# Modulation and head folds of an encoder layer issued at other places: second modulation in the Fourier stage, one side step per place

## The chip, the core and the metric

The kernel runs on one core of one Trainium2 chip. The metric is the device time of one execution in microseconds. The five engines each run their own list of instructions in order: TensorE (PE, with its weight loads as PEld), VectorE (DVE), ScalarE (ACT), GpSimd (POOL) and SyncE (SP), which issues most of the DMA transfers. All products are 32-bit; most are computed as three TensorE products of high and low parts (a value is split in two by a ScalarE copy and a VectorE subtraction).

## The reference

Two sequences of 1024 rows and 1024 columns go through one encoder layer each, with the same weights and a conditioning vector of their own:

```
mod = silu(c) @ w_ada + b_ada            # six vectors: shift, scale, gate, twice
h   = rmsnorm(x, g_mix) * (1 + sc1) + sh1
z   = h @ w_in                           # 256 q, 128 kv, 64 k_pe, 512 Fourier columns
y_mla  = attention of 4 heads from the normed q and kv latents (w_uq, w_ukv, rotary k)
y_four = real part of a 2-D DFT over sequence and 64 channels of each of 8 groups, times w_four
x   = x + ga1 * (concat(y_mla, y_four) @ w_out)
h2  = rmsnorm(x, g_ffn) * (1 + sc2) + sh2
x   = x + ga2 * ((silu(h2 @ w_gate) * (h2 @ w_up)) @ w_down)
y   = rmsnorm(x, g_final)
```

What the change touches is `mod` (an 1024 x 6144 product with two rows of c), and the weights that are prepared on the chip: `w_out` times the value part of `w_ukv` for each head, and the table of the channel DFT times the Fourier columns of `w_in`.

## The kernel before

**Prologue (0 to about 57 us).** Folded weights are made: `fold_q` (L219) for the scores, `fold_out` (L232) for the output (per head two 128 x 512 products, scaled by VectorE, stored by GpSimd's DMA queue to `wo_d`), `fold_pe` (L243). Between them run the first modulation's eight chunks: `mod_load` (L174) loads 128 rows of `w_ada` (1 MB), `mod_mm` (L182) multiplies them with silu(c), kept in `scT`, as four 32-column products. `mod_vecs` (L194) turns the summed rows into column vectors `s1`, `sh1`. The two loads of `w_out` rows for `fold_out` (L465, L470) lie between the chunk loads; the second goes to the tile `hl1`, which later takes half of `wz`.

**Stage 1 (to about 286 us).** It runs over eight pairs of row tiles (two sequences, four pairs each). `norm` (L348) loads and scales the rows (four x buffers, so two pairs), `flip` (L363) transposes them and applies shift and scale, `zproj` (L395) projects to the latents, `latents` (L425) transposes and stores them, `evenodd` (L381) and `fourier_in` (L438) make the Fourier columns with the channel table `wcs`, which `prep_wcs` (L330) makes in eight blocks of 128 rows. In `pair` (L515) the flips of the next pair are interleaved. Table blocks 0 to 3 are made ahead of the first `zproj`, blocks 4 to 7 and `norm(1)` behind it (L500 to L506).

At three places of each pair the generator `extras` (L262) is advanced; a step ends at each `yield`. It loads and multiplies the eight chunks of the gates (`cols1`), computes `small_weights`, multiplies `w_out`'s Fourier rows with the small weights and the gates into `wm_d` and `wn_d` (ten products, one step each), and at last the eight chunks of the second modulation (`cols2`), closed by `mod_vecs` for `s2`, `sh2`. Pair 0 advances it once, pairs 1 to 6 two steps at each place. Chunks pass through two 1 MB tiles (`wada`, L172).

**Fourier stage (to about 380 us).** `dft` (L619) multiplies with cosine and sine tables, `prep_wm` (L653) loads and splits `wm_d`, `fourier_out` (L689) makes the output rows in four steps per sequence and stores them to `fo_d`; then `stage3_loads` (L578) prepares the attention, which uses `wo_d` (L921) and, at its end, `s2` and `sh2` (L789). The feed-forward part begins near 890 us.

The order of the instructions on each engine is not that of the source: the tile layer places them by its own estimate of when operands and buffers are ready, and adds the waits. PSUM has eight banks of 128 x 512, shared by all products of a stage.

Of the kernel before, what the change touches and what calls it, by code (L numbers as in the profile page):

```python
# [12 lines left out]
F32 = mybir.dt.float32  # L13
# [37 lines left out]
def hybrid_encoder_kernel(ctx: ExitStack, tc: tile.TileContext, a: dict):  # L51
# [53 lines left out]
    ga_d = dram.tile([P, 512], F32, name="ga_d")  # L105
    wq_d = dram.tile([P, 2, 768], F32, name="wq_d")
# [20 lines left out]
    def rows(j, u):  # L127
        return slice(512 * u + P * j, 512 * u + P * j + P)

# [6 lines left out]
    with ExitStack() as st:  # L136
# [30 lines left out]
        nc.scalar.activation(scT[:, :, 0:2], cT, AF.Silu)  # L167

# [25 lines left out]
        def mod_vecs(mr, bcol, gi, sv, shv):  # L194
            pt = bank().rearrange("p (a b) -> p a b", a=4)
            for c in range(4):
                nc.tensor.transpose(pt[:, c, :], mr[:, c * P : (c + 1) * P], ident)
            for s in range(2):
                for j in range(2):
                    nc.vector.tensor_tensor(  # L200
                        out=shv[s][:, 4 * j : 4 * j + 4], in0=pt[:, :, 32 * j + s],
                        in1=bT[:, bcol + 4 * j : bcol + 4 * j + 4], op=ALU.add)
                    nc.vector.tensor_tensor(
                        out=sv[s][:, 4 * j : 4 * j + 4], in0=pt[:, :, 64 + 32 * j + s],
                        in1=bT[:, bcol + 8 + 4 * j : bcol + 12 + 4 * j], op=ALU.add)
                nc.vector.tensor_scalar(out=sv[s], in0=sv[s], scalar1=1.0, scalar2=None, op0=ALU.add)
                nc.vector.tensor_tensor(out=sv[s], in0=sv[s], in1=gT[:, gi, :], op=ALU.mult)

# [23 lines left out]
        def fold_out(i, wo2, wuvT, gq):  # L232
            for b in range(2):
                h = 2 * i + b
                for g in range(2):
                    gs = slice(512 * g, 512 * g + 512)
                    ps = bank()
                    nc.tensor.matmul(ps, wuvT[:, h, :], wo2[:, b, gs], start=True, stop=True)
                    so = stile("so")
                    nc.vector.tensor_scalar(out=so, in0=ps, scalar1=gq[:, 2:3], scalar2=None, op0=ALU.mult)  # L240
                    nc.gpsimd.dma_start(wo_d[:, h, gs], so)
# [20 lines left out]
        def extras():  # L262


            cols1, cols2 = [(2 * D, D), (5 * D, D)], [(3 * D, 2048)]
            wt = mod_load(0, cols1, wada_tile())
            yield
            wo4 = []
            for c in range(NC):
                nxt = mod_load(c + 1, cols1, wada_tile()) if c + 1 < NC else None  # L270
                mod_mm(1, c, wt)
                if c + 1 == NC:
                    wo4.append(wo_load(2, wada_tile()))
                    bga = stile("bga")
                    nc.sync.dma_start(bga, a["bga"])
                wt = nxt
                yield
# [4 lines left out]
            wo4.append(wo_load(3, wada_tile()))  # L282
            wo4 = [t.rearrange("p a b -> p (a b)").rearrange("p (a b) -> p a b", a=2) for t in wo4]
            yield
            for g in range(2):
# [5 lines left out]
                for p in range(5):  # L291
# [171 lines left out]
        wuvT = w.tile([P, HEADS, KVL], F32, tag="ll", name="wuvT", bufs=2)  # L463
        nc.sync.dma_start(wuvT, a["wuvT"])
        wo2 = wo_load(0, wide("hf", (P, 2, D)))  # L465
        mod_mm(0, 0, wt[0])
# [3 lines left out]
        wo2 = wo_load(1, wide("hl1", (P, 2, D)))  # L470
        wpe = w.tile([P, 2, HEADS * ROPE], F32, tag="lh", name="wpe", bufs=2)
        nc.sync.dma_start(wpe, a["wpe"])
# [3 lines left out]
        fold_out(1, wo2, wuvT, gq)  # L476
        fold_pe(wpe, gq)
# [5 lines left out]
        nc.sync.dma_start(bT, a["bT"])  # L483
        nc.sync.dma_start(gT, a["gT"])
# [25 lines left out]
        def extra(k, n):  # L510
            if k <= 6:
                for _ in range(n):
                    next(more, None)

        def pair(k):  # L515
# [11 lines left out]
            extra(k, 2 if k else 0)  # L527
            fourier_in(k, 0)
            latents(k, 1)
            extra(k, 2 if k else 1)  # L530
# [872 lines left out]
```

## Time and profile before

| | |
|---|---|
| median of 3 runs | 2242.17 us (2239.56 to 3430.17) |
| profiled execution | 2243.11 us |
| its span | 2241.3 us |
| TensorE busy | 93% |
| VectorE, ScalarE, GpSimd busy | 63%, 41%, 36% |
| mean granted TensorE clock | 0.967 |
| DMA, mean over the span | 165 GB/s |

The profile is of one execution. A busy share is an average over stages with different limits, so the lines shown below are cut by stretches of time. A line of a group of instructions gives the kernel line, engine, operation, tiles and shape, count, then the busy time in us, the mean of one in ns, and the idle time of the engine before them with what ended it. A line of the timeline gives start, duration, engine, line, operation and tiles, with the idle time before it in brackets. A line of the chain that ended last gives start, duration and what was waited for. The table of stretches gives, for each, its length, their sum, the busy time of each engine with its number of instructions, the granted TensorE clock, the DMA engines' busy share and GB/s. f32 matrix products of two passes are counted as two records.

### The profile page before, as it was taken

Reading aid. Unit: us, or ns where it says so; the run is one execution under the profiler, and the core shown is the slowest. Engines: PE = TensorE matmul, PEld = TensorE weight load, DVE = VectorE, ACT = ScalarE, POOL = GpSimd, SP = SyncE. Lnnn points to the kernel's source line nnn. Section 1 sums busy time; section 2 is a strip of 40 time slices with the busy share of each in tenths; the row PEclk is TensorE's granted clock in tenths of the full one; section 3 lists DMA queues with packets and bytes.
Section 4 is the critical chain, followed back from the end, with each engine's and each line's share of the span. In section 5 each row is a group of like instructions: output and inputs, shape, how many; then the busy total and the mean of one; then the engine's idle time right before and its main releaser. Section 6 shows DMA issues by size and latency. Waiting matters only on the chain.

```text
span 2241.3 us, 28903 instructions
## 1 busy us (share of the span) xinstructions
PE 2084.9 (93%) x10096; PEld 1692.1 (75%) x10096; DVE 1400.8 (63%) x2086; ACT 907.8 (41%) x1774; POOL 814.8 (36%) x1005
## 2 busy tenths in 40 slices
PE   5888999899999895999999999997999999999994
PEld 2666767788888784788888888885778888888883
DVE  3545565766676663776776767667566666655575
ACT  1644542555564455333332336443332332334442
POOL 1433400111223202777877730114555454410124
PEclk7999999999999997999999999999999999999997
DMA  9477546333344237454555468764333232245654
GB/s 377 162 227 222 178 154 225 91 86 86 98 133 139 97 132 228 157 176 164 194 173 184 175 201 295 230 213 159 113 118 118 94 118 94 96 154 197 222 196 141
DMA packets 183362, 370.80 MB, mean 165 GB/s; under 512 B 18928, under 2 KB 60400, under 8 KB 180144
## 3 DMA queue, kind: packets, MB, share of 16 engines
q1 hardware_dynamic: 167712, 314.68, 42.1%
q0 software_dynamic: 15504, 54.28, 7.5%
q8 instruction: 79, 1.29, 0.2%
q14 instruction: 67, 0.55, 0.1%
HBM read 257.02 MB, written 111.87 MB: 165 GB/s over the span
## 4 chain that ended last, share of the span: by engine, by line
PE 77%; DMA 7%; DVE 5%; POOL 4%; ACT 3%; issue 2%; SPq 0%; DVEq 0%; POOLq 0%; ACTq 0%
PE bank L71 21%; PE bank L73 20%; PE bank L72 20%; PE gb L71 2%; PE gb L72 2%; PE gb L73 2%; PE ppt L881 2%; DMA wada<-in_w_ada_dram 2%; PE ps_s L858 1%; PE bank L186 1%; PE ps_s L859 1%; PE ps_s L860 1%; PE ps_s L856 1%; PE ps_s L857 1%; DMA hc_d<-hcb 1%
## 5 line engine op out<-in xcount | busy, mean ns | idle before, releaser
L71 PE MATMUL bank<-H,wh 128*128 128x512 f32 x1232 | 494.3, 401 | 13.8 <-DVE val L125 6.0
L73 PE MATMUL bank<-H,wl 128*128 128x512 f32 x1232 | 487.7, 396 | 0.5 <-DVE wl L61 0.5
L72 PE MATMUL bank<-H,wh 128*128 128x512 f32 x1232 | 485.0, 394 | 0.0
L125 DVE TENSOR_TENSOR val<-bank,val 128x512 f32<-128x512 f32 x260 | 177.1, 689 | 212.0 <-PE bank L73 210.8
L61 DVE TENSOR_TENSOR wl<-draw,wh 128x512 fp32r<-128x512 f32 x308 | 213.5, 731 | 127.8 <-ACT wh L60 127.5
L71 PEld LDWEIGHTS bank<-H,wh 128*128 128x128 f32 x1232 | 232.7, 189 | 70.6 <-DVE val L125 7.3
L73 PEld LDWEIGHTS bank<-H,wl 128*128 128x128 f32 x1232 | 232.3, 189 | 61.4 <-DVE wl L61 1.2
L72 PEld LDWEIGHTS bank<-H,wh 128*128 128x128 f32 x1232 | 232.8, 189 | 55.2
L60 ACT CAST wh<-draw 128x512 fp32r<-128x512 f32 x308 | 179.3, 619 | 216.4 <-PE bank L72 173.1
L125 POOL TENSOR_TENSOR val<-val 128x512 f32<-128x512 f32 x58 | 79.9, 1383 | 507.0 <-DVE val L1227 251.3
L60 ACT CAST wh<-val 128x512 fp32r<-128x512 f32 x176 | 109.0, 622 | 361.3 <-PE bank L72 330.5
L72 PE MATMUL bank<-wl,wh 128*128 128x512 f32 x616 | 242.6, 394 | 8.9 <-DVE wl L61 8.8
L61 DVE TENSOR_TENSOR wl<-val,wh 128x512 fp32r<-128x512 f32 x176 | 193.9, 1104 | 88.0 <-ACT wh L60 87.2
L71 PE MATMUL bank<-wh 128*128 128x512 f32 x616 | 241.8, 393 | 4.5 <-ACT wh L60 4.5
L73 PE MATMUL bank<-wh,wl 128*128 128x512 f32 x616 | 241.4, 392 | 0.0
L60 ACT CAST wh<-rgu 128x512 fp32r<-128x512 f32 x132 | 81.8, 621 | 204.8 <-PE bank L72 202.0
L122 POOL TENSOR_TENSOR val<-rgu 128x512 f32<-128x512 f32 x88 | 121.2, 1379 | 98.7 <-DMA rgu<-in_wgu_dram 86.3
L72 PEld LDWEIGHTS bank<-wl,wh 128*128 128x128 f32 x616 | 116.7, 189 | 36.7 <-DVE wl L61 12.4
L71 PEld LDWEIGHTS bank<-wh 128*128 128x128 f32 x616 | 116.7, 190 | 29.6 <-ACT wh L60 5.4
L122 POOL TENSOR_TENSOR val<-rgu,val 128x512 f32<-128x512 f32 x88 | 132.4, 1505 | 7.5 <-DVE wl L61 0.7
L73 PEld LDWEIGHTS bank<-wh,wl 128*128 128x128 f32 x616 | 116.8, 190 | 24.3
L122 POOL TENSOR_TENSOR val<-val 128x512 f32<-128x512 f32 x89 | 119.6, 1360 | 1.3
(274 smaller groups left out, 3973.6 us busy)
## 6 DMA issues: line engine op xcount, KB each, us to landing
rgu<-in_wgu_dram SPq DMA_DIRECT2D x88, 512.0 KB, 4.6
draw<-s_d SPq DMA_DIRECT2D x154, 256.0 KB, 4.0
s_d<-val POOLq DMA_DIRECT2D x88, 256.0 KB, 3.7
draw<-t_d SPq DMA_DIRECT2D x88, 256.0 KB, 4.3
s_d<-val SPq DMA_DIRECT2D x66, 256.0 KB, 3.1
draw<-in_w_down_dram SPq DMA_DIRECT2D x66, 256.0 KB, 4.5
wada<-in_w_ada_dram SPq DMA_DIRECT2D x13, 1024.0 KB, 7.4
xt<-in_x_dram SPq DMA_DIRECT2D x16, 512.0 KB, 8.4
```

The lines of the kernel that those rows point to most:

```text
L60: here["a"] = nc.scalar.copy(hi, src).ins
L61: here["v"] = nc.vector.tensor_tensor(out=lo, in0=src, in1=rd(hi), op=ALU.subtract).ins
L71: nc.tensor.matmul(out, lh, rh, start=first, stop=False, skip_group_check=cont)
L72: nc.tensor.matmul(out, lh, rl, start=False, stop=False, skip_group_check=cont)
L73: nc.tensor.matmul(out, ll, rh, start=False, stop=last, skip_group_check=cont)
L122: eng.tensor_tensor(out=out, in0=x, in1=y, op=ALU.subtract)
L125: eng.tensor_tensor(out=out, in0=x, in1=y, op=ALU.add)
L186: nc.tensor.matmul(mods[key][32 * j : 32 * j + 32, :], scT[:, c, :], wt[:, j, :], start=(c == 0), stop=(c == NC - 1))
L856: nc.tensor.matmul(o, qa[0][:, us], lat[0][:, 0, gs], start=True, stop=False)
L857: nc.tensor.matmul(o, qa[0][:, us], lat[1][:, 0, gs], start=False, stop=False)
L858: nc.tensor.matmul(o, qa[1][:, us], lat[0][:, 0, gs], start=False, stop=False)
L881: nc.tensor.transpose(pt[:, c, :], p[:, (4 * g + c) * P : (4 * g + c + 1) * P], ident)
```

## The change

The second modulation leaves `extras`. Its eight chunks are loaded and multiplied in the Fourier stage, two after each of the first sequence's four `fourier_out` steps, through four tiles of its own; `scT` is stored to DRAM in the prologue and loaded again there, as are the two small tables `bT`, `gT`. `mod_vecs` becomes a function of both stages and runs after the second `dft`.

`fold_out` now takes one head. Heads 0 and 1 are folded in the prologue, as one load; heads 2 and 3 become the first steps of `extras`, in pair 0, with `wuvT` kept in another tile, and their stores go over SyncE's queue. `extras` is advanced by one step at each of the three places of every pair; two of the `wm` products make one step. All eight table blocks and `norm(1)` stand ahead of the first `zproj`, `wz_split(4)` behind the first flips, `fold_pe` and the loads of `wpe`, `bT`, `gT` earlier.

```diff
+        nc.gpsimd.dma_start(sc_d, scT)
...
-        def fold_out(i, wo2, wuvT, gq):
-            for b in range(2):
-                h = 2 * i + b
-                for g in range(2):
...
-                    nc.gpsimd.dma_start(wo_d[:, h, gs], so)
+        def fold_out(h, wo2, wuvT, gq):
+            for g in range(2):
...
+                (nc.gpsimd if h < 2 else nc.sync).dma_start(wo_d[:, h, gs], so)
...
         def extras():
-            cols1, cols2 = [(2 * D, D), (5 * D, D)], [(3 * D, 2048)]
+            cols1 = [(2 * D, D), (5 * D, D)]
+            wo2 = wo_load(1, wada_tile().rearrange("p a b -> p (a b)").rearrange("p (a b) -> p a b", a=2))
+            yield
+            fold_out(2, wo2, wuvT, gq)
             wt = mod_load(0, cols1, wada_tile())
+            yield
+            fold_out(3, wo2, wuvT, gq)
             yield
...
-                    yield
-            wt = mod_load(0, cols2, wada_tile())
-            yield
-            for c in range(NC):
-                nxt = mod_load(c + 1, cols2, wada_tile()) if c + 1 < NC else None
-                mod_mm(2, c, wt)
-                wt = nxt
-                yield
-            mr = mod_row(2)
-            yield
-            mod_vecs(mr, 24, 1, s2, sh2)
+                    if p % 2 == 1:
+                        yield
             yield
...
-        wuvT = w.tile([P, HEADS, KVL], F32, tag="ll", name="wuvT", bufs=2)
+        wuvT = w.tile([P, HEADS, KVL], F32, tag="gah1", name="wuvT")
...
         fold_out(0, wo2, wuvT, gq)
-        wo2 = wo_load(1, wide("hl1", (P, 2, D)))
...
+        fold_out(1, wo2, wuvT, gq)
+        fold_pe(wpe, gq)
...
-        wz_split(4, wz1)
-        mod_vecs(mod_row(0), 0, 0, s1, sh1)
+        mod_vecs(mod_row(0), bank, bT, gT, 0, 0, s1, sh1)
...
+        for g in range(4):
+            flip(0, g)
+        wz_split(4, wz1)
+        norm(1)
         nc.sync.dma_start(ropec, a["ropec"])
         nc.sync.dma_start(ropes, a["ropes"])
-        for g in range(4):
-            flip(0, g)
-        for i in range(4):
-            prep_wcs(i, wf[0])
+        for i in range(8):
+            prep_wcs(i, wf[i // 4])
         zproj(0, 0)
         evenodd(0)
-        for i in range(4, 8):
-            prep_wcs(i, wf[1])
-        norm(1)
...
-            extra(k, 2 if k else 0)
+            next(more, None)
...
         zsplit(1)
+        scT = wa.tile([P, NC, 32], F32, name="scT2")
+        nc.sync.dma_start(scT, sc_d)
+        bT = wa.tile([P, 48], F32, name="bT2")
+        nc.sync.dma_start(bT, a["bT"])
+        gT = wa.tile([P, 2, NC], F32, name="gT2")
+        nc.sync.dma_start(gT, a["gT"])
+        chunks = {}
+
+        def mod2(c):
+            if c + 3 < NC and c >= 0:
+                mod2_load(c + 3)
+            if c >= 0:
+                if c == 0:
+                    chunks["ps"] = bank2()
+                wt = chunks.pop(c)
+                for j in range(4):
+                    nc.tensor.matmul(chunks["ps"][32 * j : 32 * j + 32, :], scT[:, c, :], wt[:, j, :],
+                                     start=(c == 0), stop=(c == NC - 1))
+
+        def mod2_load(c):
+            chunks[c] = wa.tile([P, 4, 512], F32, tag="wada2", name="wada2", bufs=4)
+            nc.sync.dma_start(chunks[c], a["w_ada"][c * P : (c + 1) * P, 3 * D : 3 * D + 2048].rearrange("p (j n) -> p j n", n=512))
+
+        for c in range(3):
+            mod2_load(c)
         for s in range(2):
             for j in (1, 2, 3, 0):
                 fourier_out(s, abn, j)
                 if j == 1:
                     dc_prep(s, abn)
+                if s == 0:
+                    n = (1, 2, 3, 0).index(j)
+                    mod2(2 * n)
+                    mod2(2 * n + 1)
             if s == 0:
+                mr = wa.tile([P, 512], F32, name="modrow2")
+                nc.vector.tensor_copy(mr, chunks.pop("ps"))
                 abn = dft(1)
                 prep_wm(1)
+                mod_vecs(mr, bank2, bT, gT, 24, 1, s2, sh2)
                 early.close()
```

More of the change, by code (lines that the diff above doesn't have):

```diff
@@ L128, in rows, with mod_vecs @@
         return slice(512 * u + P * j, 512 * u + P * j + P)
+    def mod_vecs(mr, bank, bT, gT, bcol, gi, sv, shv):
+        pt = bank().rearrange("p (a b) -> p a b", a=4)
+        for c in range(4):
+            nc.tensor.transpose(pt[:, c, :], mr[:, c * P : (c + 1) * P], ident)
+        for s in range(2):
+            for j in range(2):
+                nc.vector.tensor_tensor(
+                    out=shv[s][:, 4 * j : 4 * j + 4], in0=pt[:, :, 32 * j + s],
+                    in1=bT[:, bcol + 4 * j : bcol + 4 * j + 4], op=ALU.add)
+                nc.vector.tensor_tensor(
+                    out=sv[s][:, 4 * j : 4 * j + 4], in0=pt[:, :, 64 + 32 * j + s],
+                    in1=bT[:, bcol + 8 + 4 * j : bcol + 12 + 4 * j], op=ALU.add)
+            nc.vector.tensor_scalar(out=sv[s], in0=sv[s], scalar1=1.0, scalar2=None, op0=ALU.add)
+            nc.vector.tensor_tensor(out=sv[s], in0=sv[s], in1=gT[:, gi, :], op=ALU.mult)
     zpool = ExitStack()
@@ L192, in mod_row @@
             return mr
[L194 to L207, printed above, removed]
         def fold_loads():
@@ L526, in pair @@
                 flip(k + 1, 3)
-            extra(k, 2 if k else 0)
+            next(more, None)
             fourier_in(k, 0)
             latents(k, 1)
-            extra(k, 2 if k else 1)
+            next(more, None)
             fourier_in(k, 1)
```

37 lines of the change are left out of this document (16 added, 21 removed).

## The prediction

> **What bounds the kernel now.** I read the page first, then busy time by stage, then TensorE's idle times, then the chain that ended last and the SyncE queue around them.
>
> ```profile
> span 2241.3 us, 28903 instructions
> PE 2084.9 (93%) x10096; PEld 1692.1 (75%) x10096; DVE 1400.8 (63%) x2086; ACT 907.8 (41%) x1774; POOL 814.8 (36%) x1005
> PE   5888999899999895999999999997999999999994
> ```
>
> TensorE is busy for 93% of the span, so a change that leaves its work alone can win only idle time and slow-clock time. The edit lies in the first eight slices (stage 1 up to about 286 us, the Fourier stage up to 380 us). Per stage:
>
> ```profile
> core 0: us, PE busy (x) PEld busy (x) DVE busy (x) ACT busy (x) POOL busy (x), PEclk, DMA share, GB/s
> 12.00:49.00 37.00, 21.70 (x81) 5.41 (x81) 10.99 (x16) 4.08 (x6) 6.83 (x15) 0.75 1.02 418
> 286.00:302.00 16.00, 14.49 (x96) 12.56 (x95) 14.64 (x32) 11.95 (x29) 0.00 (x0) 1.00 0.54 170
> 302.00:337.00 35.00, 34.64 (x146) 22.77 (x146) 23.86 (x49) 11.12 (x21) 0.00 (x0) 1.00 0.35 129
> ```
>
> To 49 us the DMA engines are saturated (share 1.02, 418 GB/s). After that TensorE is the bound, except in a few holes; the Fourier stage (302 to 337) has 0.4 us of idle TensorE and free DMA (129 GB/s). The holes, in brackets the idle time and what ended it:
>
> ```profile
> 75.77 0.66 PE L374 MATMUL bank<-ident,xt 128*128 128x128 f32 x2 [9.67 <-DVE wcs_l L343]
> 158.83 0.69 PE L374 MATMUL bank<-ident,xt 128*128 128x128 f32 x2 [6.92 <-DVE xt L360]
> 207.49 1.26 PE L186 MATMUL bank<-wada,scT 128*32 128x512 f32 x8 [4.31 <-DMA wada<-in_w_ada_dram]
> 213.80 1.06 PE L186 MATMUL bank<-wada,scT 128*32 128x512 f32 x8 [1.54 <-DMA wada<-in_w_ada_dram]
> 251.07 0.63 PE L197 MATMUL bank<-ident,modrow 128*128 128x128 f32 x4 [1.15 <-DVE modrow L191]
> 276.11 0.74 PE L431 MATMUL bank<-ident,lat 128*128 128x128 f32 x4 [1.94 <-DVE lat L416]
> 407.00 0.80 PE L856 MATMUL ps_s<-lat,qa 128*128 128x512 f32 x1 [5.53 <-ACT qa L60]
> ```
>
> Three of them leave TensorE slow behind them, by the granted clock (the last but two number):
>
> ```profile
> 77.00:78.60 1.60, 1.60 (x9) 1.55 (x8) 0.86 (x7) 1.11 (x3) 0.00 (x0) 0.53 0.05 14
> 160.00:164.50 4.50, 4.50 (x13) 2.71 (x12) 1.69 (x6) 2.60 (x6) 1.33 (x6) 0.57 0.60 160
> 406.00:413.00 7.00, 5.42 (x18) 4.44 (x19) 6.23 (x15) 3.56 (x9) 0.73 (x1) 0.51 0.21 61
> ```
>
> **The change part by part.** The sum is made against the profiled execution: 2243.11 us, a span of 2241.3 and 1.8 around it; the median shown, 2242.17, is 0.9 lower.
>
> *Prologue and pair 0.* The last modulation chunk of the prologue is awaited, and the first head folds run under it:
>
> ```profile
> 25.71 20.41 DMA wada<-in_w_ada_dram
> wo_d<-so POOLq DMA_DIRECT2D x8, 256.0 KB, 7.4
> L238 PE MATMUL bank<-wide,wuvT 128*128 128x512 f32 x16 | 9.3, 733 | 1.0 <-DMA wide<-in_w_out_dram 1.0
> L377 ACT ACTIVATE hf<-bank,sh,s 128x256 f32<-128x256 f32 x8 | 4.3, 575 | 9.7 <-PE bank L374 9.7
> L60 ACT CAST hh<-hf 128x512 fp32r<-128x512 f32 x4 | 2.6, 639 | 0.0
> L60 ACT CAST wz_h<-wide 128x896 fp32r<-128x896 f32 x2 | 1.8, 932 | 0.0
> L337 ACT CAST wcs_h<-bank 128x256 fp32r<-128x256 f32 x16 | 5.2, 403 | 0.1
> L342 ACT CAST wcs_h<-bank 128x24 fp32r<-128x24 f32 x8 | 1.4, 189 | 1.1 <-DVE wcs_l L338 1.0
> 71.47 1.09 ACT L356 ACTIVATE junk<-xt 128x1024 bf16<-128x1024 f32 x1
> 164.30 0.20 PE bank L72
> 83.01 0.44 PE bank L431 x4
> 83.44 0.87 PE bank L374 x8
> 84.07 0.37 PE L71 MATMUL bank<-wcs_h,eoh 128*128 128x280 f32 x1
> ```
>
> Taken out of the saturated stretch: one of two loads of w_out (2 x 1024 floats on 128 partitions, 1.05 MB) and four of eight 0.26 MB stores, 2.1 MB at 418 GB/s, 5.0 us, less 0.3 for the new store of scT (0.13 MB): 4.7. If the stores only overlapped the end, 2.5. I take 4, so ScalarE's first hf starts about 4 earlier, near 47.
>
> The 9.67 us hole is an order: the second square of norm(1) starts at 71.47 behind kv, which waits for GpSimd's reciprocal root; xt is scaled after it and flip(1) waits. In the changed program both squares stand ahead of kv and in the middle of the table's copies, and all eight table blocks precede the first projection. What is late next is the projection itself, which needs a PSUM bank that table block 0 releases. From 47: eight hf of 0.575, four hh of 0.64 and a wz copy of 0.93 (8.1), six table copies of 0.40 (2.4), two squares (2.1), two small copies (0.4), by the groups of ScalarE from 49 to 77 us in the fence: 60.0. Then 24 projection matmuls every 0.2 us (4.9), half a flip (0.9), the second projection (4.9), a latent flip and the other half (1.3), the first moved head fold (a quarter of 9.3, 2.3): fourier_in starts at 74.3 against 84.07, and the second fold takes another 2.3 right behind. Gain 7.5. The copy of kv and GpSimd's root still precede hf of pair 1, but that pair is due only after fourier_in. I take 7. Bounds: a loss of 2.1 (4.6 of folds exposed, only 2.5 won) and a gain of 11 (folds at full clock, hole fully closed).
>
> *One step per place, pairs 1 to 6.* Each place had two chunk steps, now one, so a chunk load has about twice the time. The SyncE queue is in order:
>
> ```profile
> 144.41 0.32 SPq L281 DMA_DIRECT2D ga_d<-modrow  x1
> 146.79 0.62 SPq L354 DMA_DIRECT2D xt<-in_x_dram  x1
> 148.43 6.13 DMA xt<-in_x_dram
> 206.47 7.29 DMA wada<-in_w_ada_dram
> DMA to landing us min/median/max: 3.8/5.3/12.8
> ```
>
> The xt of the fifth pair is issued at 146.79, behind ga_d and four latent stores, and flip waits 6.92 us for it. In the changed program that load stands ahead of the third pair's first ckv store, and ga_d a pair further back. So the 6.92 goes, and with it the slow clock: 1.2 us from 158.83 to 160 at half (0.6) and 4.5 at 0.57 (1.9): 9.4 in all. I take 9; bounds 0 (the load ends up late again) and 9.4. Each remaining chunk load is issued one to two places ahead of its use; landing takes 3.8 us at least, 5.3 in the median, 12.8 at most, and a place about 9 (some 20 of them from the fourier_in at 84 to the hole at 276), so I price these loads at 0, and at 4 if the longest meets a single place.
>
> The TensorE page of the Trainium skill ("TensorE: Matmul & The Clock Gate", Part 1) says that after an idle window of about 3.4 us the array runs at half rate until one busy window has passed. The 0.57 row agrees. Its reverse speaks against this change: by that page a newly opened hole would be charged about 1.7 us on top, as an estimate (half of 3.4).
>
> *Second modulation moved to the Fourier stage.* Stage 1 loses 32 matmul pairs and their waits:
>
> ```profile
> L186 PE MATMUL bank<-wada,scT 128*32 128x512 f32 x64 | 8.5, 615 | 5.9 <-DMA wada<-in_w_ada_dram 5.8
> ACT wm L60 <- DMA wraw<-wm_d: 1.6, 1, 1.6
> ```
>
> The 8.5 us of matmuls and 0.6 of transposes go from a TensorE-bound stretch into another: 0. The waits 4.31, 1.54 and 1.15 go: 7.0. The 1.94 in the last pair stays. In the new place 8.4 MB enter a stretch (286 to 337) that moves about 7.2 MB: 15.6 MB in 51 us is 306 GB/s, under 418. Tight is the start: four chunks (4.2 MB) beside the 2.7 MB of 286 to 302 need 431 GB/s, and chunk 0 stands on the SyncE queue ahead of the second four wm loads, for which ScalarE already waits 1.6 us; 1.05 MB at 418 is 2.5 us. TensorE enters fourier_out at 302 just behind wm. Chunks 4 to 7 are issued when the chunk four earlier is used and needed two fourier_out groups (some 14 us) later, more than 12.8. The three small loads (scT, bT, gT) wait there too; SyncE holds fo stores behind a chunk's wait only for the few matmuls before it. Twelve small VectorE instructions and one copy (about 2 us) fit in 11 idle us of 35. I charge 2; bounds 0 and 8 (wm 2.5 and its shadow, two chunk waits).
>
> "DMA: Bandwidth & Descriptors" of the Trainium skill ("Where 436 GB/s comes from") gives about 358 GB/s as what memory grants one core. The 418 row goes past it with one core alone, so the measurement decides; by 358 the first 16 us would need 19.3 and the sum would be some 3 us higher.
>
> *Attention start.* Nothing is edited there, but the order changes. Now SyncE issues two 1 MB latents ahead of the third wo_d load, and ScalarE's wv copy waits for it in front of the exponentials:
>
> ```profile
> 396.06 6.96 DMA wvr<-wo_d
> ```
>
> In the changed program the third load stands between the two latents and ScalarE meets it later. The hole of 5.53 and the clock behind it (5.42 busy at 0.51: 2.7) are 8.2. I take 4; bounds 0 and 8. The feed-forward order is the same on every engine: 0.
>
> Sum: -7 -9 -7 +2 -4 = -25. Span 2216, time 2218 against the profiled run, 2217 against the median: 1.1% faster, inside the 2% (45 us) that a measurement of this kernel can about tell from no change.
>
> **The rivals.**
> *The holes close only in part.* TensorE's order is denser and ScalarE, VectorE and GpSimd's root become what it waits for; pair 0 and the attention start give nothing and the Fourier stage costs 3. For it: the ScalarE chain I worked out for pair 0 has no slack before 60. Against: VectorE is busy 31.5 of 68 us from 77 to 145, as the row of that stretch shows:
>
> ```profile
> 77.00:145.00 68.00, 67.78 (x410) 51.05 (x409) 31.53 (x75) 36.90 (x90) 28.31 (x62) 0.99 0.59 192
> ```
>
> Time: -9 -7 +3 = -13, 2229.
> *All holes close*: -11 -9.4 -7 -8 = -35, 2207.
> *Slower: the Fourier stage waits for chunks.* Chunks 4 to 7 are issued only once a chunk is used, in the same queue as fo stores and wm loads. If landing took the longest seen, 12.8, plus the 5 us that 2 MB ahead cost at 418 GB/s, each would come 4 after the 14 us between issue and use; with 2 of slow clock behind each, four of them cost 24, and the wm loads 8: 32 against 27 won elsewhere, +5, 2247. It decides from a landing of about 17 us per chunk on. Against: the DMA share of 0.35 there.
> *The change doesn't do what it says*: the xt load or a wada load is held up behind another store, and the hole reappears in another pair: -25+16 = -9, 2233.
>
> **How the numbers follow.** Forecast 2217: 0.55. Partly closed, 2229: 0.22. All closed, 2207: 0.12. Fourier stage waits, 2247: 0.06. Hole moves, 2233: 0.05. The forecast's own spread is about 2211 to 2224. The range 2204 to 2234 takes in all but the slow rival and tails on both sides, some 0.15. Faster by over 2% means under 2197, beyond every hole of the sum: 0.04; slower by over 2% (2287) needs 70 us of new waits: 0.03; within: 0.93.
>
> **What would show it.** Right: no idle of several us before the flips of pairs 1 and 4; no TensorE wait for wada after pair 3; fourier_in of pair 0 starting near 74; stage 1 ending near 254 (the 9.1 us of moved TensorE work left it too) and the Fourier stage 9 to 11 us longer. Wrong: rows of TensorE waiting for wada in the Fourier stage, or for wm behind wraw above 3 us; a hole over 6 us in pair 0; the 5.53 us hole of the attention start unchanged.

## The result and the profile after

The changed kernel takes 2210.91 us (median of 4 runs, 2209.74 to 2212.84); the kernel before, run beside it, 2242.17 us (median of 3 runs, 2239.56 to 2243.57; a fourth run of 3430.17 us was slow and is left out, so the upper end that the table of before gives is not of these three). The ratio is 0.9863 with a 95% interval of 0.9844 to 0.9883: 1.4% faster, which is inside the 2%. The forecast was 2217 us, the range 2204 to 2234. In the profiled executions the span fell by 31.0 us where the sum had 25.

The head of the page of the changed kernel:

```profile
span 2210.3 us, 28901 instructions
PE 2076.3 (94%) x10096; PEld 1688.5 (76%) x10096; DVE 1403.0 (63%) x2086; ACT 908.9 (41%) x1774; POOL 819.9 (37%) x1002
```

TensorE has the same number of instructions and 8.6 us less busy time: part of the gain is not idle time at all. To see where it lies, the next two fences mark the same five places in both kernels' timelines of TensorE (start, duration, what it is): the first projection of pair 1, the first matmul of the Fourier stage, of the attention and of the output projection, and the last flip of h ahead of the feed-forward. Before:

```profile
93.63 0.36 PE L71 MATMUL bank<-wz_h,hh 128*128 128x448 f32 x1
...
285.68 0.39 PE L71 MATMUL bank<-tb,zh 128*128 128x258 f32 x1 [1.02 <-ACT zh L60]
...
380.62 0.39 PE L71 MATMUL gb<-wq_h,ql 128*128 128x256 f32 x1 [0.88 <-DVE ed L125]
...
455.46 0.47 PE L71 MATMUL gb<-wv,o 128*128 128x512 f32 x1
...
889.97 1.94 PE L786 MATMUL pht<-ident,xn 128*128 128x128 f32 x8 [7.64 <-DVE xn L776]
```

After, with the waits of TensorE that are left up to the attention (in brackets the idle time and what ended it):

```profile
56.41 0.61 PE L71 MATMUL bank<-wz_h,hh 128*128 128x448 f32 x1 [2.21 <-DVE wcs_l L339]
72.71 0.40 PE L71 MATMUL bank<-wcs_h,eoh 128*128 128x280 f32 x1 [0.84 <-ACT hf L373]
79.11 0.63 PE L427 MATMUL bank<-ident,lat 128*128 128x128 f32 x4 [3.05 <-DVE lat L412]
88.86 0.36 PE L71 MATMUL bank<-wz_h,hh 128*128 128x448 f32 x1
...
238.07 0.63 PE L427 MATMUL bank<-ident,lat 128*128 128x128 f32 x4 [1.44 <-DVE lat L412]
246.49 0.39 PE L71 MATMUL bank<-tb,zh 128*128 128x258 f32 x1 [1.02 <-ACT zh L60]
...
350.15 0.58 PE L71 MATMUL gb<-wq_h,ql 128*128 128x256 f32 x1 [1.60 <-DVE ed L126]
364.54 1.94 PE L901 MATMUL ppt<-ident,p 128*128 128x128 f32 x8 [2.75 <-DVE p L890]
378.87 0.79 PE L876 MATMUL ps_s<-lat,qa 128*128 128x512 f32 x1 [4.24 <-ACT qa L60]
...
426.62 0.47 PE L71 MATMUL gb<-wv,o 128*128 128x512 f32 x1
...
862.76 1.94 PE L806 MATMUL pht<-ident,xn 128*128 128x128 f32 x8 [5.84 <-DVE xn L796]
```

From one mark to the next, in us, beside what the sum had for that stretch:

| stretch | before | after | difference | forecast |
|---|---|---|---|---|
| start to pair 1 (prologue, pair 0) | 93.63 | 88.86 | -4.8 | -7 |
| pair 1 to the Fourier stage | 192.05 | 157.63 | -34.4 | -25.1 (-9, -7, -9.1 moved) |
| Fourier stage | 94.94 | 103.66 | +8.7 | +11.1 (9.1 moved, +2) |
| attention, to the first output projection | 74.84 | 76.47 | +1.6 | -4 |
| to the last flip of h | 434.51 | 436.14 | +1.6 | 0 |
| feed-forward | 1351.3 | 1347.5 | -3.8 | 0 |
| span | 2241.3 | 2210.3 | -31.0 | -25 |

So the total was near, but made of errors that cancel in part: stage 1 won 9 us more than forecast, the prologue 2 less, and the attention start did not win the 4 that were expected.

Each column is one execution, and unchanged code does not always take the same time. By the runs below that leave a stretch as it was, the first row is 87.4 to 90.1 us with the changed code and 93.6 to 95.1 with that of before, and the fourth 74.7 to 76.5 and 74.5 to 75.7. So the 1.6 us that the attention start seems to lose are not shown to be a loss, and differences of 1 to 2 us in the first row mean little.

The same stretches by windows (span of the window, then busy time of TensorE, its weight loads, VectorE, ScalarE, GpSimd, then clock, DMA share, GB/s), before:

```profile
93.63:285.68 192.05, 174.91 (x1015) 135.18 (x1013) 95.06 (x202) 88.92 (x222) 77.17 (x173) 0.96 0.65 206
285.68:380.62 94.94, 92.19 (x432) 65.14 (x433) 65.21 (x132) 34.87 (x75) 0.00 (x0) 1.00 0.50 176
```

and after:

```profile
88.86:246.49 157.63, 154.79 (x946) 128.47 (x944) 93.61 (x189) 88.52 (x222) 77.83 (x168) 1.00 0.67 199
246.49:350.15 103.66, 100.54 (x501) 67.00 (x501) 66.84 (x145) 35.45 (x75) 0.00 (x0) 1.00 0.69 244
```

From pair 1 on stage 1 now keeps TensorE busy for 154.79 of 157.63 us at full clock. The Fourier stage has 3.1 us of idle TensorE against 2.8 before: the eight chunk loads cost it nothing that can be seen. But TensorE's busy time in stage 1 fell by 20.1 us, and what moved is only 8.3: 0.6 of transposes and the chunks' matmuls, 7.7 by their own window after:

```profile
246.49:350.15 103.66, 7.70 (x64) 1.67 (x64) 1.00 0.69 244
```

### The profile page after: what moved, and what is told of

Same layout as the page of the kernel before. It is cut to its first block, busy times and chain, and to the rows that moved or that the text cites. A ratio compares the mean times of both kernels' runs of the same rounds, so it can differ in the third digit from the quotient of the medians.

```text
span 2210.3 us, 28901 instructions
## 1 busy us (share of the span) xinstructions
PE 2076.3 (94%) x10096; PEld 1688.5 (76%) x10096; DVE 1403.0 (63%) x2086; ACT 908.9 (41%) x1774; POOL 819.9 (37%) x1002
## 4 chain that ended last, share of the span: by engine, by line
PE 78%; DMA 6%; POOL 4%; DVE 4%; ACT 4%; issue 3%; SPq 0%; DVEq 0%; POOLq 0%; ACTq 0%
PE bank L71 21%; PE bank L73 21%; PE bank L72 20%; PE gb L71 2%; PE gb L72 2%; PE gb L73 2%; PE ppt L901 2%; DMA wada<-in_w_ada_dram 1%; DMA x<-in_x_dram 1%; PE ps_s L878 1%; PE ps_s L879 1%; PE ps_s L880 1%; PE ps_s L876 1%; DMA hc_d<-hcb 1%; PE ps_s L877 1%
## 5 line engine op out<-in xcount | busy, mean ns | idle before, releaser
L126 POOL TENSOR_TENSOR val<-val 128x512 f32<-128x512 f32 x58 | 81.3, 1409 | 498.8 <-DVE val L1247 329.9
L61 DVE TENSOR_TENSOR wl<-rgu,wh 128x512 fp32r<-128x512 f32 x132 | 116.4, 882 | 8.0 <-ACT wh L60 7.9
```

What stands on the lines that cost most here:

```text
L61: here["v"] = nc.vector.tensor_tensor(out=lo, in0=src, in1=rd(hi), op=ALU.subtract).ins
L126: eng.tensor_tensor(out=out, in0=x, in1=y, op=ALU.add)
```

## The experiments

**Where did 12 us of busy time go?** Slow clock is one answer (0.96 before, 1.00 after). Another stands in TensorE's timeline of the first pairs, which the prediction did not read. One such row of before and the window of the eight chunks of the gate columns (their instructions alone: span, TensorE, weight loads, clock, DMA):

```profile
121.03 1.05 PE L186 MATMUL bank<-wada,scT 128*32 128x512 f32 x4
99.00:134.00 35.00, 13.36 (x64) 2.02 (x64) 1.00 0.74 244
```

A chunk's four matmuls (x8) write 32 rows each and run side by side, 1.06 us for all. In before a chunk came by two loads, and with two steps per place the order of the program issues most chunks as two halves with other work between. Each half (x4) takes 1.05 us too. Run *b_onedma* loads each chunk by one DMA, so the four matmuls stay together:

```
         def mod_load(c, cols, wt):
+            if len(cols) == 2:
+                nc.sync.dma_start(
+                    wt.rearrange("p (k j) n -> p k j n", k=2),
+                    a["w_ada"][c * P : (c + 1) * P, :].rearrange("p (k t j n) -> p k t j n", k=2, t=3, j=2)[:, :, 2])
+                return wt
```

> The kernel before, with each chunk of the first pair's later modulation (gate and feed-forward gate columns) loaded by one DMA instead of two, so that its four matmuls stay together; nothing else is changed. Theory (split chunks): before executes these 8 chunks in 13 bursts, and a burst of half a chunk takes 1.05 us like a whole one (1.06), so 5 bursts or about 5 us go: 2238 us (2236 to 2239), and the bursts of half a chunk between 107 and 133 us are gone from TensorE's rows. Rival (the 6 us that the change won beyond the forecast came from the prologue and pair 0, and split chunks cost nothing because the two halves of the array are filled otherwise): within 1 us of before, 2242.

Measured: 2236.95 us, ratio to before 0.9987 (0.9978 to 0.9997), 2.9 us faster. The chunks' window and the wait that follows later:

```profile
93.00:134.00 41.00, 8.32 (x64) 1.36 (x64) 1.00 0.72 234
...
206.19 1.93 PE L191 MATMUL bank<-wada,scT 128*32 128x512 f32 x8 [7.83 <-DMA wada<-in_w_ada_dram]
```

The same 64 instructions take 8.32 us instead of 13.36: 5.0 us, as the theory said. Of this 3.5 came back some 70 us later: the wait for the second modulation's first chunk grew from 4.31 to 7.83 us. On the other side the second chunk is not awaited any more (1.54 us in before) and no slow clock follows the last latents (1.00 from 272 to 276), so that the Fourier stage starts 4.7 us earlier. The changed kernel issues all chunks whole (8.5 us for 64) and has no such wait left to grow. It still loads each of them by two DMAs; which part of the change keeps them together was not tried by itself. The Trainium skill, "TensorEngine Tiling (Array Packing)", Key Properties, says that tiles of the array can load and multiply in parallel; the trace agrees for the four that stand together (1.06 us), and shows that here two alone took as long (1.05 us).

**Is the fifth pair's hole SyncE's order?** Run *b_xt_early* is the kernel before with the loads of x split from `norm` and, for pairs 3 to 7, issued at the start of `pair(k)`:

```
         def pair(k):
+            if 0 < k < nk - 2:
+                norm_load(k + 2)
             if k > 0:
                 zproj(k, 0)
```

> The kernel before, with the loads of x for pairs 3 to 7 issued at the start of the pair that is two ahead of them instead of at its end; nothing else is changed. Theory (SyncE's order): the 6.92 us wait of the fifth pair's flip for xt goes and the slow clock behind it (2.5 us): 9.4 us faster, 2233 us (2232 to 2235). Rival (the transfers only trade places, and what stood ahead, the ga_d store and the w_out load, becomes late instead): a wait of several us shows elsewhere before 215 us, 2239 to 2243.

Measured: 2236.72 us, 0.9979 (0.9970 to 0.9988), 4.7 us faster. The flip does not wait any more, but the chunk does:

```profile
152.72 1.29 PE L383 MATMUL bank<-ident,xt 128*128 128x128 f32 x8
...
204.77 1.93 PE L186 MATMUL bank<-wada,scT 128*32 128x512 f32 x8 [9.97 <-DMA wada<-in_w_ada_dram]
```

The cause of the hole is confirmed; but the wait for the chunk grew by 5.7 us, and the Fourier stage starts only 5.1 us earlier. That suggested a floor: a chunk that lands at 205 to 207 us however early TensorE is. Run *b_onedma_xt* has both edits and tests it.

> The kernel before with both edits that were tried alone: one DMA per chunk of the first pair's later modulation, and the loads of x issued a pair earlier. Theory (a floor: the first chunk of the second modulation is issued on SyncE's queue behind the wm_d stores, at 199 to 203 us, and lands at 205 to 207 however early TensorE comes): the wait for it grows to 11 to 14 us, stage 1 ends no more than 6 us earlier than before, 2234 to 2237. Rival (the gains add: 3.8 and 4.4 us at the end of stage 1 in the single runs, 8 or more together): the wait stays under 9 us and the time is 2229 to 2232.

Measured: 2231.12 us, 0.9948 (0.9933 to 0.9963), 11.7 us faster; the Fourier stage starts at 274.97, 10.7 earlier than before (4.7 and 5.1 in the single runs).

```profile
198.88 1.94 PE L191 MATMUL bank<-wada,scT 128*32 128x512 f32 x8 [9.02 <-DMA wada<-in_w_ada_dram]
```

The floor falls: the wait stayed near 9 us and the chunk came 8.6 us earlier than before. So what holds it moves with TensorE. Run *b_wm_gpsimd* took one candidate out, the 32 wm_d stores on SyncE:

```
-                                nc.sync.dma_start(wm_d[s][64 * (p % 2) ...
+                                nc.gpsimd.dma_start(wm_d[s][64 * (p % 2) ...
```

> The kernel before with the 32 wm_d stores of stage 1 issued from GpSimd instead of SyncE; nothing else is changed. Theory (the floor is SyncE's queue of wm_d stores, 0.6 to 0.9 us each): the second modulation's first chunk is issued 5 us or more earlier and the waits of 4.31 and 1.54 us go: 5 to 7 us faster, 2235 to 2237. Rival (the chunk waits for its buffer, the last reader of w_out's rows, or for the memory): it is issued or lands at the same time, within 2 us of before, or slower where GpSimd's additions come late behind its own DMA issues.

Measured: 2250.03 us, 1.0035 (1.0023 to 1.0047): 8 us slower. TensorE's timeline, GpSimd's, and the chain that ended last:

```profile
165.03 0.69 PE L374 MATMUL bank<-ident,xt 128*128 128x128 f32 x2 [13.04 <-DVE xt L360]
216.30 1.94 PE L186 MATMUL bank<-wada,scT 128*32 128x512 f32 x8 [3.44 <-DMA wada<-in_w_ada_dram]
```

```profile
153.98 3.22 POOL L304 DMA_DIRECT2D wm_d<-so  x6 [4.50 <-DVE so L301]
159.47 1.03 POOL L304 DMA_DIRECT2D wm_d<-so  x2 [2.27 <-DVE t L413]
160.58 0.22 POOL L93 TENSOR_SCALAR rs_v<-ms 128x2 f32<-128x2 f32 x1
```

```profile
202.62 3.54 PE bank L297 x8
209.20 7.05 DMA wada<-in_w_ada_dram
```

The theory falls: neither the chunk nor the kernel came earlier, and the rival fits, on its slower side. GpSimd takes its queue in order: behind the stores, which wait for VectorE's products, stands the reciprocal root of the next norm, so the flip of the fifth pair waits 13.04 us instead of 6.92. TensorE itself is late by that, so the run does not tell what the wm_d stores alone cost in before. And the chunk still waits: its buffer holds w_out's rows until the last small product ends at 206.16, its load is issued at 209.20, behind a store of latents on SyncE's queue, and TensorE has it at 216.30. In before, TensorE's last small product and SyncE's queue read:

```profile
195.83 3.62 PE L297 MATMUL bank<-wada,lw 128*24 128x512 f32 x8
...
201.64 0.90 SPq L307 DMA_DIRECT2D wn_d<-so  x2
202.63 0.36 SPq L177 DMA_DIRECT2D wada<-in_w_ada_dram  x1
```

There the buffer is free at 199.45, and the load is issued 3.2 us later, behind stores of latents and of wn_d; in *b_xt_early* it is 7.7 us later (191.08 and 198.82). So the late chunk of before has two causes close together, the buffer and then the stores ahead of the load on SyncE; which of these stores would have to go is not shown.

**What is the new place of the second modulation worth?** Run *a_mod2_stage1* is the changed kernel with the modulation back at the end of stage 1, two steps per place from the fifth pair on:

```
+            cols2 = [(3 * D, 2048)]
+            wt = mod_load(0, cols2, wada_tile())
+            yield
+            for c in range(NC):
+                nxt = mod_load(c + 1, cols2, wada_tile()) if c + 1 < NC else None
+                mod_mm(2, c, wt)
...
+        def extra(k):
+            for _ in range(2 if k >= 4 else 1):
+                next(more, None)
```

> The changed kernel, with the second modulation put back at the end of stage 1 (two steps per place in the last three pairs) and out of the Fourier stage. Theory by the sum's terms (waits 7.0 in stage 1, a charge of 2 in the Fourier stage): 4 to 6 us slower than the changed kernel, 2215 to 2217, with TensorE rows waiting for wada after 190 us. Second theory (the chunk loads in the Fourier stage delay the fo stores and so the attention start by 3 to 4 us): the waits of stage 1 return but the start of the attention wins 3 to 4, in sum 0 to 3 slower, 2211 to 2214. Rival (with whole chunks and one queue order these waits do not return): 2 to 4 us faster than the changed kernel, 2207 to 2209.

Measured: 2222.71 us, 0.9915 (0.9899 to 0.9932) of before, 11.8 us above the changed kernel's median.

```profile
206.29 1.94 PE L202 MATMUL bank<-wada,scT 128*32 128x512 f32 x8 [9.93 <-DMA wada<-in_w_ada_dram]
362.66 0.38 PE L71 MATMUL gb<-wq_h,ql 128*128 128x256 f32 x1 [0.88 <-DVE ed L126]
```

All three theories had too little. The wait for the first chunk is back, at 9.93 instead of 4.31, since the other edits had made TensorE early for it. The attention starts at 362.66, 12.5 later than in the changed kernel. The stretch from there to the output projection, 74.53 us, is 1.9 shorter than in the changed kernel's profile, but only 0.2 shorter than the shortest of the same code.

**The two parts of the prologue.** Run *a_table_late* puts the end of the prologue back in the old order, *a_folds_prologue* puts the folds of heads 2 and 3 back:

```
-        norm(1)
...
-        for i in range(8):
-            prep_wcs(i, wf[i // 4])
+        for i in range(4):
+            prep_wcs(i, wf[0])
         zproj(0, 0)
         evenodd(0)
+        for i in range(4, 8):
+            prep_wcs(i, wf[1])
+        norm(1)
```

> The changed kernel with the order of the prologue's end as before: table blocks 4 to 7 and the second pair's norm stand behind the first projection. Theory (the table-first order closed the 9.67 us hole of pair 0): a hole of 8 to 10 us returns ahead of the flip of pair 1 and the two small ones (2.21 and 3.05) go with it: 4 to 7 us slower than the changed kernel, 2215 to 2218. Rival (the new holes and the slow clock behind them ate what the order won, and only the earlier end of the prologue's loads counts): within 2 us of the changed kernel, 2209 to 2213.

```
+        wo2 = wo_load(1, wide("hl1", (P, 2, D)))
         mod_mm(0, 2, wt[0])
         mod_mm(0, 3, wt[1])
...
+        fold_out(2, wo2, wuvT, gq)
+        fold_out(3, wo2, wuvT, gq)
         norm(0)
```

> The changed kernel with the folds of heads 2 and 3 back in the prologue, their w_out rows loaded between the modulation chunks and their four stores on GpSimd's queue. Theory (the folds are exposed for 4.6 to 5.4 us in pair 0, and the loads that they need under the saturated start cost 5.0 to 5.5): the two cancel, within 1.5 us of the changed kernel, 2209.5 to 2212.5, with the first scaled h near 50.5 instead of 45.6. Rival 1 (the folds fill holes of pair 0 that stay when they are gone): 3 to 5 us slower, 2214 to 2216. Rival 2 (the stores only overlap the end of the loads, 2.5 us): 2 to 3 us faster, 2208 to 2209.

*a_table_late* measured 2211.40 us, 0.9865 (0.9851 to 0.9880): the same as the changed kernel. The hole is back, and pair 1 starts no later:

```profile
66.79 0.66 PE L370 MATMUL bank<-ident,xt 128*128 128x128 f32 x2 [7.73 <-DVE xt L356]
...
88.54 0.36 PE L71 MATMUL bank<-wz_h,hh 128*128 128x448 f32 x1
```

Its rival holds: the table-first order traded one hole of 7.73 us for 2.21, 0.84 and 3.05 and slow clock, and won nothing. *a_folds_prologue* measured 2215.52 us, 0.9891 (0.9874 to 0.9907), a median 4.6 above the changed kernel's:

```profile
49.93 1.08 PE L134 MATMUL bank<-ident,modrow 128*128 128x128 f32 x4 [0.90 <-DVE modrow L208]
...
84.43 0.66 PE L424 MATMUL bank<-ident,lat 128*128 128x128 f32 x2 [6.36 <-DVE lat L409]
...
92.61 0.36 PE L71 MATMUL bank<-wz_h,hh 128*128 128x448 f32 x1
```

Its first rival fits best, though the interval just touches that of the changed kernel (up to 0.9883), and the profiled execution, its fastest, is only 0.4 us above that of the changed kernel. The loads end 5.9 us later again (49.93 against 44.02), and without the folds the wait for the latents in pair 0 is 6.36 us instead of 3.05: the folds fill half of a hole. Pair 1 starts at 92.61 against 88.86 (87.4 to 90.1 with the same code), so most of the 4.8 us of the prologue is the folds' move, 3.8 by these two executions. Run *a_fill* lets the second fold fill the rest of the hole:

```
             fourier_in(k, 0)
+            if k == 0:
+                next(more, None)
             latents(k, 1)
-            next(more, None)
+            if k > 0:
+                next(more, None)
```

> The changed kernel with the fold of head 3 ahead of the second flip of latents in pair 0, instead of behind it. Theory (the 3.05 us wait for the latents is idle time in which the 2.7 us fold fits, and without the wait TensorE keeps its clock behind it): the wait falls under 0.6 us and the time by 3 to 4 us, 2207 to 2208. Rival (what is won in pair 0 is given back before the end of stage 1 or at the attention's seams): the wait goes, but the time is within 1.5 us, 2209.5 to 2212.5.

Measured: 2210.48 us, 0.9862 (0.9846 to 0.9879), no change that can be told. The wait is 1.47 instead of 3.05, not under 0.6, and pair 1 starts at 86.71, 2.1 earlier. The loads of the prologue happened to end later in this execution (45.42 against 44.02), so that from their end to pair 1 it is 3.6 us less, as expected; but the rival holds, for the time does not show it.

```profile
80.05 0.66 PE L427 MATMUL bank<-ident,lat 128*128 128x128 f32 x4 [1.47 <-DVE lat L413]
```

**Why did the attention start not win?** SyncE's timeline shows the loads of the attention's first tensors (ql ahead of all) behind two fo stores of the second sequence in the changed kernel:

```profile
321.45 0.99 SPq L705 DMA_DIRECT2D fo_d<-ed  x2
322.62 0.37 SPq L563 DMA_DIRECT2D ql<-lat_d  x1
```

That is 27.5 us ahead of the attention's first matmul. In before it was 32.1:

```profile
348.48 0.88 SPq L575 DMA_DIRECT2D ql<-lat_d  x2
```

Run *a_loads_first* moves the modulation's vector steps behind these loads:

```
-                mod_vecs(mr, bank2, bT, gT, 24, 1, s2, sh2)
                 early.close()
...
                 wq_h, wq_l, rc, rs = stage3_loads()
+                mod_vecs(mr, bank2, bT, gT, 24, 1, s2, sh2)
```

> The changed kernel, with the modulation's small tensors kept in the longer-lived pool and its vector steps put behind the loads of the attention's first tensors, so that SyncE issues these loads ahead of the second sequence's fo stores, as in the kernel before. Theory (in the changed kernel these loads, 3.9 MB, start 4.6 us later against the end of the Fourier stage than before, run into the fo stores and the wvr loads and cost the attention start 3 us): ql is issued at least 4 us earlier, the wait ahead of the first flip of probabilities falls from 2.75 to under 2, and the time is 2 to 3.5 us lower than that of the changed kernel, 2207 to 2209. Rival (the loss at the attention start comes from the wvr loads alone, behind x in the queue): ql earlier, but the time within 1 us, 2210 to 2212.

Run *a_wvr4* takes the other suspect, the chain of wo_d loads through two shared half tiles:

```
-                if s == 0:
-                    raw = half("wvr")
-                elif h == 0:
-                    raw4 = e.tile([P, 4, 512], F32, tag=f"lat0{g}", name="wvr4")
-                if s == 1:
-                    raw = raw4[:, h, :]
+                if h == 0:
+                    raw4 = (e if s else w).tile([P, 4, 512], F32, tag=f"lat{1 - s}{g}", name="wvr4" if s else "wvr")
+                raw = raw4[:, h, :]
```

> The changed kernel, with the first sequence's wo_d quarters loaded into the memory of the second sequence's latents (not needed before the 27th step of the attention) instead of two shared half tiles, so that all eight loads are issued without waiting for a buffer. Theory (the start of the attention hangs on the chain of the wvr loads, 8.37 us in one of them): the 4.24 us idle of TensorE ahead of the scores shrinks below 1.5, and the slow clock behind it goes: 5 to 7 us faster than the changed kernel, 2204 to 2206. Rival (ScalarE and VectorE are the bound there: exponentials, splits of wv and probabilities; or the 4 MB issued together hold up the latents and x): the hole only moves, 2209 to 2213.

*a_loads_first* measured 2210.22 us, 0.9860 (0.9846 to 0.9875); *a_wvr4* 2211.08 us, 0.9864 (0.9849 to 0.9879). TensorE of the first and then of the second:

```profile
361.47 1.06 PE L901 MATMUL ppt<-ident,p 128*128 128x128 f32 x8 [1.88 <-DVE p L890]
375.51 0.79 PE L876 MATMUL ps_s<-lat,qa 128*128 128x512 f32 x1 [6.71 <-ACT qa L60]
```

```profile
365.93 1.94 PE L901 MATMUL ppt<-ident,p 128*128 128x128 f32 x8 [3.91 <-DVE p L890]
377.69 0.50 PE L876 MATMUL ps_s<-lat,qa 128*128 128x512 f32 x1 [1.70 <-ACT qa L60]
```

With the loads first, SyncE issues ql 32.0 us ahead of the attention's first matmul (317.00, in the row below), the wait ahead of the flip is 1.88 instead of 2.75 and the flip runs at full clock (1.06 instead of 1.94 us), and the stretch to the output projection is 74.98 us; but the wait for the scores is 6.71. None of this is clear of what the unedited code does: in *a_table_late*, *a_folds_prologue* and *a_fill* ql is issued only 27 us ahead, and the wait ahead of the flip is 1.96, 1.63 and 2.34 us, the flip at full clock each time, the wait for the scores 5.32, 5.09 and 6.69, and the stretch 74.92, 74.68 and 76.20. That the later loads cost anything is thus not shown. With own memory for wo_d the scores wait 1.70 instead of 4.24, while the flip waits 3.91, and the stretch falls to 72.95, below all of these. So the chain of wo_d loads is a real loss of the attention start. Neither edit shows in the time: both theories miss it, and both rivals fit.

```profile
317.00 0.89 SPq L563 DMA_DIRECT2D ql<-lat_d  x2
```

What the chain of wo_d loads does can be read on ScalarE, which copies a wo_d quarter right ahead of the exponentials and of qa, for which the scores wait. Before and after, with its own wait in brackets:

```profile
404.45 0.62 ACT L60 CAST wv<-wvr 128x512 fp32r<-128x512 f32 x1 [5.11 <-POOL wvr L929]
...
376.83 0.62 ACT L60 CAST wv<-wvr 128x512 fp32r<-128x512 f32 x1 [3.39 <-POOL wvr L949]
```

Both together, *a_both*, and with the fold as well, *a_all*:

> The changed kernel with both edits: the attention's loads ahead of the fo stores, and the wo_d quarters of the first sequence in the memory of the second sequence's latents. Theory (two separate losses, 2 to 3.5 and 3.7 us as seen at 390 us in the run with the wo_d edit alone): TensorE is 5 to 7 us ahead of the changed kernel at the fourth head of the attention, and the time is 2204 to 2206. Rival (VectorE, not TensorE, is the bound at the seams between the sequences and at the end of the attention, as the run with the wo_d edit alone gave back 2 of its 4 us between 700 and 850): ahead at the fourth head, but 2208 to 2210 at the end.

> The changed kernel with three edits: the fold of head 3 ahead of the second flip of latents in pair 0, the attention's first loads ahead of the fo stores, and the wo_d quarters in the memory of the second sequence's latents. Theory (gains of separate places, 3 to 4 in pair 0 and 1 to 6 at the attention start): 2203 to 2207, below every run of the changed kernel's median. Rival (VectorE bounds the attention's end, so nothing won before it counts in full): 2207 to 2210.

Measured: *a_both* 2210.04 us, 0.9856 (0.9841 to 0.9871); *a_all* 2207.23 us (2203.66 to 2210.53), 0.9841 (0.9825 to 0.9857).

*a_both* misses the 2204 to 2206 of its theory. *a_all* has the lowest ratio of all, 3.7 us under the changed kernel's median, but the intervals overlap, so that it beats the changed kernel is likely and not shown. The stretch to the output projection is 71.22 us in *a_both* and 72.13 in *a_all*, 4 to 5 below the changed kernel's profile and at least 2.5 below the shortest of the same code without these edits. What follows it blurs such gains: with the same code, the stretch from there to the last flip of h takes 434.5 to 437.5 us and the feed-forward 1346.2 to 1351.3 in the fourteen profiled executions of this study. Whether VectorE takes back what TensorE wins, as the rival had it, is therefore open.

## Why the prediction was right, and where its terms were wrong

**Prologue and pair 0 (-7): mis-sized, -4.8, and by another split.** The loads ended 5 us earlier (4 taken), and 3.8 of the gain are the folds' move by the two executions compared. The step that failed is the closed 9.67 us hole: I let everything behind it move up and priced only one new wait, the table's bank. TensorE met that one (2.21, at 56.41 instead of 60.0), and then two that I had not listed, 0.84 and 3.05, with slow clock behind the first and the last of the three (0.57 from 56 to 60, 0.66 from 80 to 85). *a_table_late* shows that the order won nothing.

**xt of the fifth pair (-9): right in cause and price in its place.** *b_xt_early* shows it in before alone: the wait of 6.92 us is gone and the clock is 1.00 behind the flip (152.7 to 158). What the step missed is that half of the price comes back at the second modulation's first chunk as long as that stands in stage 1. The terms -9 and -7 were added as if independent; they did add only because the change removes the place where one would be paid back.

**Second modulation (-7 of waits, +2 of charge): too small on both sides.** The waits went, and the slow clock behind 4.31 us too, which I had not priced (0.61 of full clock from 207.4 to 211, 1.4 us). The wait for latents at the end of stage 1 was to stay at 1.94; it fell to 1.44, and no slow clock follows it now (0.57 from 276 to 280, some 1.7 us). The charge of 2 did not come: 103.66 less 94.94 is 8.7 us for 8.3 of moved work. With the other edits in place this part is worth 11.8 us (*a_mod2_stage1*).

**Gate chunks, one step per place (0): the step that missed most, -5.0.** I priced their loads and not their matmuls. The sum took "x64, 8.5 us" for moved chunks and did not look at the other 64, which took 13.36. *b_onedma* shows the 5.0 us.

**Attention start (-4): the gain did not come.** I saw that the third wo_d load would stand between the latents and took this for a gain. The step that failed is that ScalarE would meet this load later and the hole would halve. ScalarE still waits for a wo_d quarter right ahead of the exponentials, 3.39 us against 5.11, and the scores wait 4.24 us, and 5.09 to 6.69 in the three other executions with the same code, against 5.53: the sign of being wrong that I had named for this step came true. *a_wvr4* shows that the chain of loads through two half tiles holds it: without it the scores wait 1.70. I also read the order on SyncE only around wo_d: 27 us ahead of the attention the stage's first loads fall behind two fo stores, since the pool whose memory they reuse closes only behind the moved modulation's vector steps; and ScalarE copies wo_d's first quarter at 360.27, ahead of the first exponentials, where in before the exponentials came first. *a_loads_first* turns both orders back, but that they cost time is not shown. The +1.6 after the attention start and the -3.8 in the feed-forward lie within what the same code varies by.

**The rivals.** The holes did close only in part in pair 0 and at the attention, with some 10 us of missed items on the other side (5.0 of split chunks, 3.6 of the two waits' clock and length, 1.6 of the charge). By the time alone, 2210.91 us is nearer to the rival in which all holes close (2207) than to the forecast (2217), and at the lower edge of the spread of about 2211 to 2224; but that rival is not what happened, for holes of 3.05 and 4.24 us stayed. So the forecast came near in part by luck: what it missed on one side made up for what it overrated on the other. The slower rival did not occur: no matmul of TensorE waits for wada in the Fourier stage (one weight load does, 0.4 us), the chunks landed in 8.2 us in the median, and the 17 us from which it would have decided was far. Of the signs named, the flips, the absence of wada, and fourier_in of pair 0 (72.71 against 74.3) came as written, and so did the unclosed hole of the attention start among those of being wrong; stage 1 ended at 246.5 rather than 254.

## What to carry to other kernels

Gains that close waits on one engine are not to be added row by row: ask for each what TensorE meets next when it comes early, because in this kernel about half of a closed hole came back at the next late load until that load was moved as well. Look at the busy time of small matmuls that share the array and not only at idle time, since a burst split in two cost twice. And follow every pool that closes behind moved work: the loads that reuse its memory move too, whether or not that costs time, which was not shown here.

## What the runs showed of the hardware

Two matmuls of 32 columns take as long as four that stand together: 1.05 against 1.06 us. Eight chunks cost 13.36 us when split and 8.32 when whole, at full clock in both.

The slow clock does not follow a fixed length of idle time. Before, 1.94 us of idle time at 276 us was followed by 0.57 of the clock:

```profile
276.00:280.00 4.00, 3.89 (x19) 3.92 (x20) 2.21 (x8) 1.41 (x6) 2.25 (x8) 0.57 0.54 138
```

In *a_fill* 2.34 us ahead of a flip were not: its eight transposes took 1.06 us, where they take 1.94 at a clock of 0.50 (364.54 in the changed kernel), and the granted clock was 1.00 from 362.60 to 366.60.

```profile
362.61 1.06 PE L904 MATMUL ppt<-ident,p 128*128 128x128 f32 x8 [2.34 <-DVE p L893]
```

The Trainium skill, "TensorE: Matmul & The Clock Gate", Part 1, has the clock follow an activity window of about 3.4 us that runs freely, which would allow both; the runs do not show the window itself.
